# A hybrid decoder layer on one core: x tiles 2048 bytes apart, token sums for two units at a time, one weight sum by DMA, first gated tiles loaded under the up product

## The chip, the cores and the metric

The kernel runs on one core of a Trainium2 chip. TensorE (PE) multiplies, VectorE (DVE), ScalarE (ACT) and GpSimd (POOL) work on whole tiles, SyncE (SP) starts most DMAs. The metric is device time of one execution in microseconds, lower is better; the figure for a kernel is the median of its runs. A matmul's form is written "128*128 128x512": 128x128 weights against a moving tile of 128 rows and 512 columns.

## The reference

One layer, batch 1, 512 tokens, width 2048, all float32, in three sub-layers with a residual each: a mixer of three head groups, a cross-attention into 256 memory tokens, and a gated MLP with a causal convolution of width 3 over the gate. The change is in the seam from the second to the third, in the third, and in how the tiles of activations are laid out everywhere.

```python
def memory_cross_attention(h, mem_n, w_q, w_kv, w_o):
...
    o = jnp.einsum('bhsm,bmhd->bshd', p.astype(v.dtype), v).reshape(B, S, CROSS_WIDTH)
    return o @ w_o

def conv_ffn(h, w_up, conv_w, conv_b, w_down):
    S = h.shape[1]
    val, gate = jnp.split(h @ w_up, 2, axis=-1)
    gp = jnp.pad(gate, ((0, 0), (CONV_W - 1, 0), (0, 0)))
    g = conv_b
    for i in range(CONV_W):
        g = g + conv_w[i] * gp[:, i:i + S]
    return (jax.nn.silu(g) * val) @ w_down

...
        x = x + hybrid_mixer(rms_norm(x, norm_mix[l]), w_in[l], f_bias[l], rel_table,
                             c_gate_w2[l], c_gate_b[l], c_norm[l], w_out[l])
        x = x + memory_cross_attention(rms_norm(x, norm_cross[l]), mem_n, w_cq[l], w_ckv[l], w_co[l])
        x = x + conv_ffn(rms_norm(x, norm_ffn[l]), w_up[l], conv_w[l], conv_b[l], w_down[l])
    return rms_norm(x, norm_final)
```

The width of the MLP is 5504, that is 43 tiles of 128.

## The kernel before

**Three matmuls for one.** Every float32 operand is split into a hi and a lo part of a type that PE takes faster. `mm3` adds hi·hi (L352), hi weights · lo activations (L353) and lo weights · hi activations (L354) in PSUM. The hi part is an ACT copy, the lo part a DVE subtraction. For weights that is `split_weights` (ACT L313, DVE L314) or `weights` (ACT L338, DVE L339): a raw tile `wraw` of 128x1024 (512 KB; `WR` = 5 buffers) becomes two halves, each with one of `WS` = 5 buffers `whi` and `wlo`. An element-wise operation that PE waits for is therefore nearly always a split.

**Activations** are kept as 16 pairs of tiles `xhi`, `xlo` (`xslot`), 512 columns of 4 bytes, each tile padded to 528 columns, so that neighbours start 2112 bytes apart. Other pools hold `coh`/`col` (the attention's output) and `gh`/`gl` (some of the gated tiles) without padding, 2048 bytes apart.

**The w_co stage** (end of `cross()`): eight units u. Each loads 512 KB of weights, does two chains of 12 matmuls 128x512, adds the result to the residual stream (`resid`, DVE L959) and to the sums of squares (`square`, L983: ACT squares, DVE and POOL take turns in adding), and calls `token_sums(u)`.

**Strassen.** The up product is done by seven products of half-size blocks instead of eight. Per unit u, `token_sums` scales two tiles (y0, y1), takes their halves of 256 tokens as a11, a21, a12, a22, makes four sums of them (DVE L1150), and splits all seven (ACT L1159, DVE L1160), 128x256 each. That makes 56 tiles of [hi | lo]; 32 lie in the slots of `xhi` and `xlo`, the others in pools of their own as `sum`. A table `SHIFT` shifts each unit's content within its tile by 0 to 14 elements.

**`up()`**: 43 rounds f. A round loads four blocks of weights (b11, b12, b22, b21, 512 KB each), makes the weight sums in four DVE operations of 128x1024 (L1193, temporaries t1, t2), and does the products in the order 1, 6, 5, 7, 4, 2, 3, each with 24 matmuls 128x256 (8 units times 3), 168 in all. The results become `val` (the value half) and `gp` (the gate), the convolution and the gate follow on ACT and DVE (L1226 to L1229, then a multiplication, L1193), and the gated tile is stored to DRAM as `gd` (SP, L1232). In the first round the norm's factor `R` is worked out too.

**The down product** (`ffn()`): `load` reads a gated tile back (`graw`, SP L1250), splits it (ACT L1258, DVE L1259) into an x slot or into `gh`/`gl`; its first group of units uses tiles 0 to 3, in two units of 24 matmuls 128x512, then tiles 4 to 7 and so on.

**What sets the order.** Each engine takes its instructions in one order, which a scheduler fixes when the program is built, near the order of the code; an instruction that waits holds all behind it on its engine. SP's DMAs are such a queue too: a load that is behind a store which waits for its data starts after it.

Of the kernel before, what the change touches and what calls it, by code (L numbers as in the profile page):

```python
# [47 lines left out]
GB_SLOTS = 10  # L48
SHIFT = (0, 1, 2, 4, 6, 8, 12, 14)
LEVELS = (64, 32, 16, 8, 4, 2, 1)  # L50
# [161 lines left out]
class _Trunk:  # L212
# [774 lines left out]
    def cross(self):  # L987
# [127 lines left out]
        wx = self.pool(es_w, "wx", "right")  # L1115
        self.sums = []
        for u in range(8):
            w = self.weights(d["w_co"][u])
            pss = [self.acc(), self.acc()]
            for half in range(2):  # L1120
                for k in range(4):
                    wh, wl = w((half * 4 + k) * P, P)
                    self.mm3(pss[half], wh, wl, oT[k][0], oT[k][1], k == 0, k == 3)
                dt = 2 * u + half
                self.resid(dt, pss[half], self.x1[dt], sqs, lambda n: wx.tile([P, n], F32, name="xsqt", tag="xsqt", bufs=2))
            if u == 7:
                es_o.close()
                self.es_fa = ExitStack()
                sx = self.pool(self.es_fa, "fa", "left")
            self.sums.append(self.token_sums(u, sx, wx))  # L1130
        es_w.close()

    def token_sums(self, i, pool, tmp):

        nc = self.nc
        y = []
        for e in range(2):
            t = tmp.tile([P, S], F32, name="y%d" % e, tag="y%d" % e, bufs=2)
            nc.scalar.activation(t, self.x1[2 * i + e], AF.Copy, scale=self.gain(2, 2 * i + e))
            y.append(t)  # L1140
        a11, a21 = y[0][:, :HT], y[0][:, HT:]
        a12, a22 = y[1][:, :HT], y[1][:, HT:]
        s = [tmp.tile([P, HT], F32, name="s%d" % n, tag="s%d" % n, bufs=2) for n in range(1, 5)]
        src = {1: a11, 6: s[1], 5: s[0], 7: s[2], 4: a22, 2: a12, 3: s[3]}
        made = {5: (a21, a22, ALU.add), 6: (s[0], a11, ALU.subtract), 7: (a11, a21, ALU.subtract),
                3: (a12, s[1], ALU.subtract)}
        out = {}
        for n, j in enumerate((1, 5, 6, 7, 4, 2, 3)):
            if j in made:
                nc.vector.tensor_tensor(src[j], made[j][0], made[j][1], op=made[j][2])  # L1150
            slot = 7 * i + n
            if slot < 2 * KT:
                tag = ("xhi", "xlo")[slot % 2]
                t = self.xp.tile([P, S + 16], F32R, name=tag, tag=tag, bufs=KT)
            else:
                t = pool.tile([P, S + 16], F32R, name="sum%d" % slot)
            o = SHIFT[i]
            th, tl = t[:, o:o + HT], t[:, o + HT:o + S]
            nc.scalar.activation(th, src[j], AF.Copy)  # L1159
            nc.vector.tensor_tensor(tl, src[j], th.bitcast(F32), op=ALU.subtract)  # L1160
            out[j] = (th, tl)
        return out

    def up(self):

        nc, d = self.nc, self.d
        es = ExitStack()
        fb = self.pool(es, "fb", "right")  # L1170
        gps = [fb.tile([P, S + 2], F32, name="gp%d" % i) for i in range(2)]
        for g in gps:
# [5 lines left out]

        def raw(u):
            t = self.wp.tile([P, 1024], F32, name="wraw", tag="wraw", bufs=WR)  # L1180
            nc.sync.dma_start(out=t, in_=d["w_up"][u])
            return t

        def product(j, w, ps, start, stop):
            for h in range(2):
                th, tl = self.split_weights(w[:, h * 512:(h + 1) * 512])
                for k in range(4):
                    i, c = 4 * h + k, slice(k * P, (k + 1) * P)
                    self.mm3(ps, th[:, c], tl[:, c], *self.sums[i][j], start and i == 0, stop and i == NP - 1,
                             more=True)  # L1190

        def tt(out, a, b, op):
            nc.vector.tensor_tensor(out, a, b, op=op)  # L1193

        def one(f):
            b11, b12, b22, b21 = [raw(4 * f + i) for i in range(4)]
            pa, pb = self.acc()[:, :HT], self.acc()[:, :HT]
            pc, pd = self.pst("C")[:, :HT], self.pst("D")[:, :HT]
            s1, u2, u3 = [fb.tile([P, HT], F32, name=n, tag=n, bufs=1) for n in ("s1", "u2", "u3")]
            val = fb.tile([P, S], F32, name="val", tag="val", bufs=1)  # L1200
            gp = gps[f % 2]
            product(1, b11, pa, True, True)
            nc.scalar.activation(s1, pa, AF.Copy)
            t1 = fb.tile([P, 1024], F32, name="t1", tag="t1", bufs=1)
            t2 = fb.tile([P, 1024], F32, name="t2", tag="t2", bufs=1)
# [3 lines left out]
            tt(u2, pb, s1, ALU.add)  # L1209
            product(5, t1, pc, True, True)  # L1210
            if f == 0:
                self.R = self.rms(self.sqs, S, self.con)
            tt(b12, b22, b12, ALU.subtract)
            product(7, b12, pb, False, True)
            tt(u3, pb, s1, ALU.add)
            tt(gp[:, 2 + HT:], pc, u3, ALU.add)
            tt(t2, t2, b21, ALU.subtract)
            product(4, t2, pd, True, True)
            tt(val[:, hi], u3, pd, ALU.subtract)
            product(2, b21, pa, False, True)  # L1220
            nc.scalar.activation(val[:, lo], pa, AF.Copy)
            product(3, b22, pc, False, True)
            tt(gp[:, 2:2 + HT], pc, u2, ALU.add)
            tt(gp[:, 2:], gp[:, 2:], self.R, ALU.mult)
            c = fb.tile([P, S], F32, name="cv", tag="cv", bufs=2)
# [7 lines left out]

        self.gd = {}
        for f in range(FT):
# [5 lines left out]
    def ffn(self):  # L1241
# [3 lines left out]
        fp = self.pool(es, "fp", "right")  # L1245
        gT = {}

# [147 lines left out]
```

## Time and profile before

| | us |
|---|---|
| median of 3 runs | 2411.97 (2410.82 to 2414.61) |
| the profiled execution, whole | 2413.33 |
| its span in the trace | 2411.5 |
| mixer, and cross-attention up to its output product | 0 to 974.5 |
| w_co stage with token sums | 974.5 to 1032.2 |
| up(), 43 rounds | 1032.2 to 1904.9 |
| seam without matmuls | 1904.9 to 1914.2 |
| down product, end | 1914.2 to 2411.5 |

The clock that PE was granted is 0.991 of full on average. A row of the profile reads: line, engine, operation, output<-inputs with their form, count, then busy time and the mean of one in ns, then the idle time of the engine before them and what ended it. In a row of one tile, three durations stand for the least, the middle and the greatest in ns, then the first and the last start in us. In a timeline, a row has start, duration, engine and instruction; matmuls overlap, so that the next starts before the last ends, and their pace is read from start to start. PEld is the loading of weights beside the matmuls. DMA rows give KB and the median time from issue to landing.

### The profile page before, as it was taken

How to read it: one execution, taken by the hardware profiler on the slowest of the kernel's cores; microseconds unless marked ns; L12 is line 12 of the kernel's file. 1: busy time of each engine (PE TensorE's matmuls, PEld its weight loads, DVE VectorE, ACT ScalarE, POOL GpSimd, SP SyncE). 2: the span in 40 equal slices, each digit the busy share in tenths (PEclk: the TensorE clock that was granted, in tenths of full speed). 3: DMA queues.
4: the chain of work that ended last, by engine and by line, in shares of the span. 5: the costliest groups of instructions: out<-in, count | busy, mean ns of one | idle time of the engine just before them, and what ended most of it. 6: DMA issues, size and time to landing. Idle time of an engine off the chain costs nothing.

```text
span 2411.5 us, 37909 instructions
## 1 busy us (share of the span) xinstructions
PE 2360.5 (98%) x14514; PEld 2119.6 (88%) x14514; DVE 1657.7 (69%) x3112; ACT 1140.8 (47%) x2185; POOL 88.2 (4%) x91
## 2 busy tenths in 40 slices
PE   9999999999999999889999999999999899999997
PEld 8798898888878888689999999999999788888887
DVE  7726656667785365888888888888888733343336
ACT  6323346555664264655555555555555522232223
POOL 2000000000001000100000000000000000000003
PEclk9999999999999999989999999999999999999999
DMA  6432132222224352123333333333333533242332
GB/s 206 145 95 83 47 105 80 96 89 94 86 91 149 119 161 80 60 94 119 119 119 119 119 119 119 119 119 119 119 119 119 184 104 120 96 158 96 109 103 73
DMA packets 87458, 269.15 MB, mean 112 GB/s; under 512 B 9788, under 2 KB 14540, under 8 KB 87276
## 3 DMA queue, kind: packets, MB, share of 16 engines
q1 hardware_dynamic: 79504, 254.64, 32.9%
q10 hardware_dynamic: 7772, 12.09, 1.5%
q8 instruction: 114, 1.87, 0.3%
q14 instruction: 68, 0.56, 0.1%
HBM read 251.18 MB, written 19.45 MB: 112 GB/s over the span
## 4 chain that ended last, share of the span: by engine, by line
PE 93%; DVE 3%; ACT 2%; DMA 1%; POOL 1%; issue 0%; DVEq 0%; SPq 0%; POOLq 0%; ACTq 0%
PE acc L352 18%; PE acc L354 18%; PE acc L353 18%; PE psC L353 3%; PE psC L352 3%; PE psC L354 3%; PE acc L393 3%; PE acc L395 3%; PE acc L394 3%; PE psD L353 2%; PE psD L354 2%; PE psD L352 2%; PE psU L354 2%; PE psV L354 2%; PE psU L353 2%; PE psV L353 2%
## 5 line engine op out<-in xcount | busy, mean ns | idle before, releaser
L339 DVE TENSOR_TENSOR wlo<-wraw,whi 128x512 fp32r<-128x512 f32 (+2 forms) x496 | 336.8, 683 | 427.4 <-ACT whi L338 418.8
L338 ACT ACTIVATE whi<-wraw 128x512 fp32r<-128x512 f32 (+2 forms) x496 | 304.5, 617 | 643.5 <-PE acc L353 381.9
L352 PE MATMUL acc<-xhi,whi 128*128 128x512 f32 (+1 forms) x1518 | 554.4, 365 | 14.8 <-ACT xhi L1258 9.0
L354 PE MATMUL acc<-xhi,wlo 128*128 128x512 f32 (+1 forms) x1518 | 548.8, 362 | 0.0
L353 PE MATMUL acc<-xlo,whi 128*128 128x512 f32 (+1 forms) x1475 | 535.7, 363 | 0.0
L352 PEld LDWEIGHTS acc<-xhi,whi 128*128 128x128 f32 x1518 | 286.8, 189 | 56.6 <-ACT xhi L1258 9.2
L354 PEld LDWEIGHTS acc<-xhi,wlo 128*128 128x128 f32 x1518 | 287.4, 189 | 46.0 <-issue 0.8
L353 PEld LDWEIGHTS acc<-xlo,whi 128*128 128x128 f32 x1475 | 278.8, 189 | 43.5 <-issue 0.9
L313 ACT ACTIVATE whi<-wraw 128x512 fp32r<-128x512 f32 x344 | 215.7, 631 | 201.2 <-PE acc L353 70.3
L314 DVE TENSOR_TENSOR wlo<-wraw,whi 128x512 fp32r<-128x512 f32 x344 | 232.3, 686 | 34.0 <-ACT whi L313 32.7
L313 ACT ACTIVATE whi<-t 128x512 fp32r<-128x512 f32 x258 | 162.9, 633 | 160.2 <-PE acc L353 97.0
L314 DVE TENSOR_TENSOR wlo<-t,whi 128x512 fp32r<-128x512 f32 x258 | 173.5, 687 | 40.0 <-ACT whi L313 39.2
L352 PE MATMUL acc<-sum,whi 128*128 128x256 f32 x559 | 157.8, 282 | 0.9 <-ACT sum L1159 0.9
L353 PE MATMUL acc<-sum,whi 128*128 128x256 f32 x559 | 157.9, 283 | 0.5 <-DVE sum L1160 0.5
L354 PE MATMUL acc<-sum,wlo 128*128 128x256 f32 x559 | 157.3, 281 | 0.0
L353 PE MATMUL acc<-xhi,whi 128*128 128x256 f32 x430 | 121.6, 283 | 0.0
L393 PE MATMUL acc<-whi,xhi 128*128 128x384 f32 (+2 forms) x320 | 114.8, 359 | 1.0 <-ACT whi L338 0.6
L395 PE MATMUL acc<-whi,xlo 128*128 128x384 f32 (+2 forms) x320 | 112.6, 352 | 0.4 <-DVE xlo L306 0.4
L394 PE MATMUL acc<-wlo,xhi 128*128 128x384 f32 (+2 forms) x320 | 112.3, 351 | 0.0
L352 PE MATMUL acc<-xlo,whi 128*128 128x256 f32 x387 | 109.5, 283 | 0.0
L354 PE MATMUL acc<-xlo,wlo 128*128 128x256 f32 x387 | 109.3, 282 | 0.0
L353 PEld LDWEIGHTS acc<-sum,whi 128*128 128x128 f32 x559 | 106.0, 190 | 0.7 <-DVE sum L1160 0.7
(369 smaller groups left out, 5245.0 us busy)
## 6 DMA issues: line engine op xcount, KB each, us to landing
wraw<-in_w_up SPq DMA_DIRECT2D x172, 512.0 KB, 3.8
wraw<-in_w_dn SPq DMA_DIRECT2D x80, 512.0 KB, 3.7
wraw<-in_w_o SPq DMA_DIRECT2D x32, 512.0 KB, 3.6
wraw<-in_w_qka SPq DMA_DIRECT2D x24, 512.0 KB, 3.7
gd<-cv SPq DMA_DIRECT2D x43, 256.0 KB, 4.3
graw<-gd SPq DMA_DIRECT2D x43, 256.0 KB, 4.4
wraw<-in_w_qkb SPq DMA_DIRECT2D x16, 512.0 KB, 3.8
xraw<-in_xT SPq DMA_DIRECT2D x15, 512.0 KB, 3.8
```

Of the source, the lines that this page charges most:

```text
L313: nc.scalar.activation(hi, r, AF.Copy)
L314: nc.vector.tensor_tensor(lo, r, hi.bitcast(F32), op=ALU.subtract)
L338: nc.scalar.activation(hi, r, AF.Copy)
L339: nc.vector.tensor_tensor(lo, r, hi.bitcast(F32), op=ALU.subtract)
L352: nc.tensor.matmul(out, lh, rh, start=start, stop=False, skip_group_check=more)
L353: nc.tensor.matmul(out, lh, rl, start=False, stop=False, skip_group_check=more)
L354: last = nc.tensor.matmul(out, ll, rh, start=False, stop=stop, skip_group_check=more)
L393: self.nc.tensor.matmul(o, xh[:, tt], wh, start=(k == 0), stop=False)
L394: self.nc.tensor.matmul(o, xh[:, tt], wl, start=False, stop=False)
L395: self.last = self.nc.tensor.matmul(o, xl[:, tt], wh, start=False, stop=(k == KT - 1))
```

## The change

It has five parts.

1. `xslot` no longer pads: x tiles are 512 columns, 2048 bytes, apart. The table `SHIFT` becomes the constant 8, for the sums in pools of their own.
2. `token_sums` handles two units at once (v = 0 to 3, called after each odd u): y tiles of [128, 2, 512], sums and splits of 128x2x256. The sums are stored by product: `sums[j, v]` holds a hi tile and a lo tile with two units each. Products 1, 5, 2, 6 lie in the x slots, the others as `sh`/`sl` in pools. Some sums have another sign, and the results are combined accordingly. The w_co weights are split two units ahead.
3. After unit 6, the first two weight blocks of round 0 are loaded and b11 split; after unit 7, b11 + b12 is made and split, before the last token sums.
4. In `up()` the products run in the order 1, 5, 2, 6, 3, 4, 7. The weight sums are made in place: b11 += b12, += b22, += b21 on DVE, and b22 += b12 by an accumulating DMA from POOL's queue, which reads b12 again from DRAM, in two halves of 256 KB. b22 has two buffers of its own (pool `fb`).
5. In the last round, gated tiles 0 to 3 are read into two `wraw` buffers and split into x slots before the products end; `load` then starts with tile 4. The DMA scratch memory grows from 1024 to 2048 bytes.

```diff
@@
-        hi = self.xp.tile([P, n], F32R, name="xhi", tag="xhi", bufs=KT, padded_shape=[P, S + 16])
-        lo = self.xp.tile([P, n], F32R, name="xlo", tag="xlo", bufs=KT, padded_shape=[P, S + 16])
+        hi = self.xp.tile([P, n], F32R, name="xhi", tag="xhi", bufs=KT, padded_shape=[P, S])
+        lo = self.xp.tile([P, n], F32R, name="xlo", tag="xlo", bufs=KT, padded_shape=[P, S])
@@ cross(), the w_co stage
-            w = self.weights(d["w_co"][u])
+            w = ws[u]
...
+            if u + 2 < 8:
+                ws.append(self.weights(d["w_co"][u + 2]))
+            elif u == 6:
+                first = [self.up_raw(i) for i in range(2)]
+                self.first = [first, self.halves(first[0])]
+            else:
+                nc.vector.tensor_tensor(first[0], first[0], first[1], op=ALU.add)
+                self.first.append(self.halves(first[0]))
...
-            self.sums.append(self.token_sums(u, sx, wx))
+            if u % 2:
+                self.token_sums(u // 2, wx)
@@ token_sums
+        def part(j):
             if j in made:
                 nc.vector.tensor_tensor(src[j], made[j][0], made[j][1], op=made[j][2])
...
+            th, tl, o = self.sums[j, v]
+            th, tl = [t[:, o:o + S].rearrange("p (i c) -> p i c", c=HT) for t in (th, tl)]
             nc.scalar.activation(th, src[j], AF.Copy)
             nc.vector.tensor_tensor(tl, src[j], th.bitcast(F32), op=ALU.subtract)
...
+        for j in UP_ORDER:
+            part(j)
@@ new
+    def halves(self, w, add=None):
+
+        parts = []
+        for h in range(2):
+            c = slice(h * 512, (h + 1) * 512)
+            parts.append(self.split_weights(w[:, c]))
+            if add is not None:
+                self.nc.gpsimd.dma_start(out=w[:, c], in_=self.d["w_up"][add][:, c], accum_op=ALU.add)
+        return parts
@@ up(), one round
-            tt(t1, b12, b11, ALU.subtract)
-            tt(t2, b22, t1, ALU.subtract)
-            product(6, t2, pb, True, True)
...
+            if f:
+                tt(b11, b11, b12, ALU.add)
+                w5 = self.halves(b11)
+            product(5, w5, pc, True, True)
+            nc.scalar.activation(s5, pc, AF.Copy)
+            product(2, self.halves(b21), pa, False, True)
...
+            tt(b11, b11, b22, ALU.add)
+            product(6, self.halves(b11), pb, True, True)
...
+            product(3, self.halves(b22, 4 * f + 1), pc, False, True)
...
+            tt(b11, b11, b21, ALU.add)
+            product(4, self.halves(b11), pd, True, True)
+            if f == FT - 1:
+                self.early = [self.wp.tile([P, 2, S], F32, name="wraw", tag="wraw", bufs=WR) for _ in range(2)]
+                for i, t in enumerate(self.early):
+                    for k in range(2):
+                        nc.sync.dma_start(out=t[:, k, :], in_=self.gd[2 * i + k])
+            product(7, self.halves(b22), pb, False, True)
+            if f == FT - 1:
+                for i in range(FB):
+                    src = self.early[i // 2][:, i % 2, :]
+                    self.gT[i] = self.xslot()
+                    nc.scalar.activation(self.gT[i][0], src, AF.Copy)
+                    nc.vector.tensor_tensor(self.gT[i][1], src, self.gT[i][0].bitcast(F32), op=ALU.subtract)
```

How this moves instructions, at two places. A row is line, operation, output<-inputs and form; numbers behind a name tell tiles of one name apart. The lines are those of each kernel's own code: after the change, L1175 and L1179 are the sums and splits in `token_sums`, L316 the weight splits, L1227 the sums of weights and results.

DVE from the last unit's token sums to the first weight splits of `up()`, before:

```order
L1160 TENSOR_TENSOR sum_9950<-s_9942,sum_9950 128x256
L1160 TENSOR_TENSOR sum_9958<-s_9944,sum_9958 128x256
L1160 TENSOR_TENSOR sum_9954<-s_9943,sum_9954 128x256
L1160 TENSOR_TENSOR sum_9961<-y_9940,sum_9961 128x256
L1160 TENSOR_TENSOR sum_9964<-y_9940,sum_9964 128x256
L1150 TENSOR_TENSOR s_9945<-y_9940,s_9943 128x256
L1160 TENSOR_TENSOR sum_9968<-s_9945,sum_9968 128x256
L1193 TENSOR_TENSOR t_10028<-wraw 128x1024
L1193 TENSOR_TENSOR t_10029<-wraw,t_10028 128x1024
L1193 TENSOR_TENSOR wraw<-wraw 128x1024
L314 TENSOR_TENSOR wlo<-t_10029,whi 128x512 x2
L314 TENSOR_TENSOR wlo<-t_10028,whi 128x512 x2
```

The same place after the change, from the third split of the last pair of units on:

```order
L1179 TENSOR_TENSOR xlo<-y_9865,xhi 128x512
L1175 TENSOR_TENSOR sb<-sa,y_9862 128x512
L1179 TENSOR_TENSOR sl_9859<-y_9865,sh_9858 128x512
L1175 TENSOR_TENSOR sa<-y_9862 128x512
L1179 TENSOR_TENSOR xlo<-sb,xhi 128x512
L316 TENSOR_TENSOR wlo<-wraw,whi 128x512
L1175 TENSOR_TENSOR sb<-sb,y_9865 128x512
L1179 TENSOR_TENSOR sl_9861<-sa,sh_9860 128x512
L316 TENSOR_TENSOR wlo<-wraw,whi 128x512
L1179 TENSOR_TENSOR sl_9857<-sb,sh_9856 128x512
L1227 TENSOR_TENSOR wraw<-wraw,b_9892 128x1024
L316 TENSOR_TENSOR wlo<-wraw,whi 128x512 x2
```

Before, three operations of 128x1024 stand between the last sum and the splits of the weights that follow. After, one stands there, the sums are twice as wide, and two splits of a block that needs no sum stand among them.

SP from the last rounds of `up()` to the down product, before (`gd<-cv` stores of the last two rounds, `wraw<-in_w_dn` the down weights, `graw` the gated tiles read back, beginning with tile 0):

```order
L1181 DMA wraw<-in_w_up 128x1024
L327 DMA wraw<-in_w_dn 128x1024 x3
L1232 DMA gd_21001<-cv 128x512
L327 DMA wraw<-in_w_dn 128x1024 x4
L1232 DMA gd_21263<-cv 128x512
L1250 DMA graw<-gd_10259 128x512
L1250 DMA graw<-gd_10521 128x512
```

The same place after the change (`L1269` reads back tiles 0 to 3; the stores belong to the last three rounds, and `graw` begins with tile 4):

```order
L1269 DMA wraw<-gd_10156 128x512
L1288 DMA gd_20676<-cv 128x512
L1269 DMA wraw<-gd_10419 128x512
L1269 DMA wraw<-gd_10682 128x512
L1269 DMA wraw<-gd_10945 128x512
L329 DMA wraw<-in_w_dn 128x1024 x2
L1288 DMA gd_20939<-cv 128x512
L329 DMA wraw<-in_w_dn 128x1024 x6
L1288 DMA gd_21224<-cv 128x512
L329 DMA wraw<-in_w_dn 128x1024
L1306 DMA graw<-gd_11208 128x512
L1306 DMA graw<-gd_11471 128x512
```

Before, the first read of a gated tile stands behind the last store. After, four reads stand two stores earlier, and tile 4 stands behind the last store and one more load of down weights.

More of the change, by code (lines that the diff above doesn't have):

```diff
@@ L1142, in token_sums @@
[L1142 to L1148, printed above, removed]
+        a11, a21 = y[0][:, :, :HT], y[0][:, :, HT:]
+        a12, a22 = y[1][:, :, :HT], y[1][:, :, HT:]
@@ L1149, in token_sums @@
+        sa, sb = [tmp.tile([P, 2, HT], F32, name=n, tag=n, bufs=1) for n in ("sa", "sb")]
+        src = {1: a11, 2: a12, 4: a22, 5: sa, 6: sb, 3: sb, 7: sa}
+        made = {5: (a22, a21, ALU.subtract), 6: (sa, a11, ALU.add), 3: (sb, a12, ALU.subtract),
+                7: (a21, a11, ALU.subtract)}
+        def part(j):
             if j in made:
                 nc.vector.tensor_tensor(src[j], made[j][0], made[j][1], op=made[j][2])
[L1151 to L1156, printed above, removed]
@@ L1177, in cw, with product @@
             return self.conv[:, i * FT + f:i * FT + f + 1]
[L1179 to L1190, printed above, removed]
+        def product(j, parts, ps, start, stop):
+            for i in range(NP):
+                th, tl = parts[i // 4]
+                c = slice(i % 4 * P, (i % 4 + 1) * P)
+                sh, sl, o = self.sums[j, i // 2]
+                m = slice(o + i % 2 * HT, o + (i % 2 + 1) * HT)
+                self.mm3(ps, th[:, c], tl[:, c], sh[:, m], sl[:, m], start and i == 0, stop and i == NP - 1, more=True)
@@ L1197, in one @@
             pa, pb = self.acc()[:, :HT], self.acc()[:, :HT]
             pc, pd = self.pst("C")[:, :HT], self.pst("D")[:, :HT]
[L1199 to L1200 removed]
+            s1, s5, u2, u3 = tmp("s1"), tmp("s5"), tmp("u2"), tmp("u3")
+            val = tmp("val", S, 2)
             gp = gps[f % 2]
[L1202 removed]
+            if f:
+                w1 = self.halves(b11)
```

82 lines of the change are left out of this document (50 added, 32 removed).

## The prediction

> **What bounds the kernel now.** I read first the page's busy times and its chain, then a table by stretch of time, and last the single gaps.
>
> ```profile
> PE 2360.5 (98%) x14514; PEld 2119.6 (88%) x14514; DVE 1657.7 (69%) x3112; ACT 1140.8 (47%) x2185; POOL 88.2 (4%) x91
> PE 93%; DVE 3%; ACT 2%; DMA 1%; POOL 1%; issue 0%; DVEq 0%; SPq 0%; POOLq 0%; ACTq 0%
> ```
>
> PE is busy for 98% of the span and holds 93% of the chain. So time can come from two places: from the pitch of the matmuls (start to start, with nothing between), or from the few stretches in which PE waits. The table by stretch shows the second kind.
>
> ```profile
> core 0: us, PE busy (x) PEld busy (x) DVE busy (x) ACT busy (x) POOL busy (x), PEclk, DMA share, GB/s
> 974.50:1032.20 57.70, 46.76 (x182) 35.73 (x182) 52.32 (x111) 39.21 (x88) 12.60 (x8) 0.91 0.17 55
> 1032.20:1064.20 32.00, 24.53 (x174) 23.45 (x173) 29.02 (x48) 18.76 (x35) 1.44 (x3) 0.84 0.24 77
> 1064.20:1084.20 20.00, 20.00 (x171) 20.00 (x170) 17.74 (x28) 11.69 (x19) 0.00 (x0) 1.00 0.38 127
> 1904.90:1914.20 9.30, 0.31 (x4) 0.10 (x2) 4.10 (x8) 4.03 (x6) 0.00 (x0) 0.73 0.49 167
> ```
>
> The first row is the `w_co` stage, the second the first of the 43 rounds of `up()`, the third a settled round, the fourth the seam between `up()` and the down product. In a settled round PE is never idle. In the first two stretches DVE is busy for 81.34 of 89.70 us while PE idles for 18.4 of them and the granted clock falls to 0.91 and 0.84: DVE is the bound there. At the seam no engine is: 9.3 us pass in a chain of short steps.
>
> **The change, part by part.**
>
> *(a) x tiles 2048 bytes apart.* The trace has both layouts side by side in the down product: `xhi`/`xlo` lie 2112 bytes apart before, `gh`/`gl`, from another pool, 2048.
>
> ```profile
> L352 PE MATMUL psU<-gh,whi x40: 388/389/397, 1966.8 to 2338.4; 128*128 128x512 f32 x40
> L352 PE MATMUL psU<-xhi,whi x120: 387/393/399, 1922.4 to 2356.5; 128*128 128x512 f32 x120
> ```
>
> ```profile
> 1995.65 0.39 PE L354 MATMUL acc<-gh,wlo 128*128 128x512 f32 x1
> ...
> 1999.73 0.39 PE L354 MATMUL acc<-gh,wlo 128*128 128x512 f32 x1
> ...
> 2000.18 0.40 PE L353 MATMUL psU<-xlo,whi 128*128 128x512 f32 x1
> ...
> 2011.54 0.39 PE L354 MATMUL psU<-xhi,wlo 128*128 128x512 f32 x1
> ```
>
> From 1995.65 to 1999.73 lie 18 pitches on `gh`/`gl`: 226.7 ns each. From 2000.18 to 2011.54 lie 49 on `xhi`/`xlo`: 231.8 ns. The medians (the middle of the three durations) differ by 4 ns, 389 against 393, the pitches by 5. How many matmuls have such tiles:
>
> ```profile
> L352 PE MATMUL acc<-xhi,whi 128*128 128x512 f32 x1056 | 423.7, 401 | 9.0 <-ACT xhi L1258 9.0
> L354 PE MATMUL acc<-xhi,wlo 128*128 128x512 f32 x1056 | 418.0, 396 | 0.0
> L353 PE MATMUL acc<-xlo,whi 128*128 128x512 f32 x1056 | 417.3, 395 | 0.0
> L352 PE MATMUL psV<-xhi,whi 128*128 128x512 f32 x120 | 47.2, 393 | 0.0
> ```
>
> That is 3168, and with 120 on each of three lines for both `psU` and `psV`, 3888. At 4 ns they give 15.6 us. The least duration on `xhi`, 387, says that some run at the short pitch already, so I take **14**. The ends: nothing, if the pool and not the spacing makes the difference; 19.8 at 5.1 ns. A loss is possible too: in the new layout a hi tile and its lo tile are exactly 32768 bytes apart, a distance that no row of before shows; by the gap between the two layouts I bound it at 14 us the other way.
>
> A page speaks against this term. The Trainium skill, "TensorE: Matmul & The Clock Gate", section "Part 2: What happens when you issue a matmul", gives the matmul's moving operand and the weight load independent read ports and a fixed 216 ns between 512-wide matmuls, so spacing should not count; the trace has 226.7 and 231.8 instead of one figure. By that rule the term would be 0.
>
> *(b) Token sums in pairs of units, and the first weights before them.* Per unit, DVE before has 2 residual adds, 2 weight splits, on average 0.9 adds of squares, and 11 sums and splits 256 wide.
>
> ```profile
> L959 DVE TENSOR_TENSOR str<-acc,str 128x512 f32<-128x512 f32 x7 | 4.7, 684 | 2.0 <-PE acc L354 2.0
> L1160 DVE TENSOR_TENSOR sum<-s,sum 128x256 fp32r<-128x256 f32 x9 | 3.6, 416 | 0.0
> ```
>
> Over eight units: 39 operations of 512 at 0.684 and 88 of 256 at 0.416, 63.3 us, against 192 matmuls at 0.227, 43.6, on PE. After: 39 + 44 of 512, all at 0.684, 56.8. DVE remains the bound and saves **6.5**. Then the start of `up()`:
>
> ```profile
> 1035.76 0.38 PE L352 MATMUL acc<-sum,whi 128*128 128x256 f32 x1 [0.92 <-ACT sum L1159]
> 1036.64 0.38 PE L353 MATMUL acc<-sum,whi 128*128 128x256 f32 x1 [0.50 <-DVE sum L1160]
> 1036.86 0.28 PE L354 MATMUL acc<-sum,wlo 128*128 128x256 f32 x1
> 1042.95 0.58 PE L352 MATMUL acc<-xhi,whi 128*128 128x256 f32 x1 [5.81 <-ACT whi L313]
> ```
>
> ```profile
> L1193 DVE TENSOR_TENSOR t<-wraw 128x1024 f32<-128x1024 f32 x43 | 52.8, 1227 | 1.4
> L1160 DVE TENSOR_TENSOR sum<-s,sum x13: 411/414/426, 1015.7 to 1039.4; 128x256 fp32r<-128x256 f32 x13
> 1040.00:1048.00 8.00, 4.80 (x20) 4.51 (x21) 7.97 (x10) 4.16 (x7) 0.00 (x0) 0.50 0.20 66
> ```
>
> The last split of a sum starts at 1039.4; behind it on DVE stand three weight sums of 1.23 us (3.7 in all), which product 6 needs, and PE stands still for 5.81 us, then runs at half clock (0.50 from 1040 to 1048). In the changed order the splits of products 1 and 5 are done before the last sums, the sums come in the order in which products use them, and product 2 needs no weight sum. The first round took 32.0 where a settled one takes 20.0. What is late next are the last four units' worth of sums, 11 operations of 0.684 or 7.5 us behind the last residual add, of which product 1 needs the first only and each later product 2.9 us later. I leave 5.5 of the 12.0 us standing and take **6.5**. Together (b) is 13. The ends: nothing (DVE gains nothing by wide operations), and 26.1, which is all that both stretches hold: 89.7 less 43.6 less 20.0.
>
> *(c) Weight sums in place, one by DMA.* The pace of a settled round:
>
> ```profile
> L352 PE MATMUL psD<-xhi,whi x86: 278/280/281, 1055.6 to 1897.1; 128*128 128x256 f32 x86
> ACT whi L313 <- PE acc L353: 156.7, 194, 0.8
> L1193 DVE TENSOR_TENSOR gp<-gp,R x43: 684/686/694, 1066.4 to 1905.7; 128x512 f32<-128x512 f32 x43
> L1228 DVE SCALAR_TENSOR_TENSOR cv<-gp,conv,cv x43: 743/746/752, 1070.1 to 1908.0; 128x512 f32<-128x512 f32 x43
> ```
>
> From 1055.6 to 1897.1 are 42 rounds, 20.04 us each: 168 matmuls at 119.3 ns. ACT, which feeds them, waits for PE to free a weight buffer (156.7 us on that row alone, from 1100 to 1900), so PE sets the pace. Per round the change takes one weight sum (1.23 us) from DVE, exchanges the 0.69 of `gp<-gp,R` for a 0.75 operation of the kind in the last row, and gives ACT one more 256-wide copy. All of it lies under PE: **0**. Only a new pitch of the 256-wide matmuls could move it; 1.2 ns either way would be 9 us over 7224 matmuls, and that is the end I keep. The DMA on POOL's queue is a new wait. Half n of `b22` is issued after DVE's split of it in product 3 and read again four halves later, in product 7. A half is 12 matmuls, 1.43 us; ACT sees the DMA after 3 halves, 4.3 us, and PE, with three halves of lead in the five buffers, after 8.6.
>
> ```profile
> wraw<-in_w_up SPq DMA_DIRECT2D x172, 512.0 KB, 3.8
> graw<-gd SPq DMA_DIRECT2D x43, 256.0 KB, 4.4
> ```
>
> No such transfer is in the trace. The nearest rows land in 3.8 and 4.4 us; I take 4.4 for 256 KB, hence nothing, and keep as the bad end twice that, 8.8, since it reads its target as well. The Trainium skill, "DMA: Bandwidth & Descriptors", section "Anatomy of one DMA — SWDGE (gpsimd) path", has 2.0 us plus the bytes by 436 GB/s, an estimate of 2.6 us here, for plain transfers; by it the term is 0 as well, and no run here shows it yet.
>
> *(d) Four gated tiles under up.*
>
> ```profile
> 1904.89 0.28 PE L354 MATMUL psC<-sum,wlo 128*128 128x256 f32 x1
> 1914.16 0.80 PE L352 MATMUL acc<-xhi,whi 128*128 128x512 f32 x1 [8.99 <-ACT xhi L1258]
> ...
> 1919.32 0.42 PE L354 MATMUL acc<-xhi,wlo 128*128 128x512 f32 x1
> ```
>
> ```profile
> 1910.19 0.33 SPq L1232 DMA_DIRECT2D gd<-cv  x1
> 1910.57 4.61 SPq L1250 DMA_DIRECT2D graw<-gd  x8
> ...
> 1913.48 1.31 ACT L1258 ACTIVATE xhi<-graw 128x512 fp32r<-128x512 f32 x2 [2.74 <-DMA graw<-gd]
> ...
> L1258 ACT ACTIVATE xhi<-graw 128x512 fp32r<-128x512 f32 x30 | 18.3, 626 | 6.7 <-DMA graw<-gd 4.9 <-PE psV L354 1.2
> L1259 DVE TENSOR_TENSOR xlo<-graw,xhi 128x512 fp32r<-128x512 f32 x30 | 20.2, 690 | 6.7 <-ACT xhi L1258 6.6
> ```
>
> PE stands from 1905.01 to 1914.16 because the loads of the gated tiles stand behind the last round's store in SP's queue, and then does 12 matmuls in 5.16 us, at half clock, where 12 × 0.232 is 2.8. That is 9.15 + 2.4 = 11.5. After, tiles 0 to 3 wait ready, which is 48 matmuls or 11 us of work at 0.23. Tile 4 decides what is left. In SP's order one more load of down weights now stands between the last store and tile 4. It takes the fifth-last `wraw` buffer, which is free once the eighth half of down weights is split, and that split needs a `whi` buffer that PE gives up after three halves, 36 matmuls or 8.3 us into the down product. With 0.6 and 0.7 us of splitting, tile 4's load starts some 9.7 us after `up()` ends, lands 2.9 later as the first `graw` did (issued at 1910.57, ACT's wait for it over at 1913.48) and needs 0.63 more until PE can begin: 13.2 to 14.7 with the median landing of 4.4, against the 11.0 that are covered. PE stands for 2.2 to 3.7 us and may run a few matmuls at half clock. I leave 4.5 of the 11.5 standing, 3 of idling and 1.5 of low clock, and take **7**; ends 0 and 11.5.
>
> The two loads per round more (0.5 MB beside 2.5) and the larger DMA scratch get nothing: SP's loads are issued a round ahead.
>
> **Sum.** Against the profiled execution, 2413.3 (span 2411.5 and 1.8 around it; the median of the runs, 2412.0, is 1.3 less): 2413.3 − 14 − 13 − 0 − 7 = **2379**.
>
> **Rivals.**
> 1. *Spacing buys nothing.* For it: `gh` and `xhi` are also of different pools. Against: PE does the same instructions at the same weights within 5 us of each other. Then 2413.3 − 20 = 2393. The rule of the Trainium skill, "TensorE: Matmul & The Clock Gate", quoted under (a) has the same result.
> 2. *DVE stays the bound of the seam into up.* For it: DVE at 52.32 of 57.70 us, and still 56.8 of work to do; the first weights' splits now stand ahead of the last sums. If half of (b) comes, 2386; if none, 2392.
> 3. *The accumulating DMA is late.* PE loses in each of 43 rounds what the transfer takes over 8.6 us. Place: ACT's split of `b22` in product 7. The other gains, 34, are used up at 34 / 43 = 0.8 us, so from 9.4 us on the kernel is slower; at 10 us it takes 2379 + 60 = 2439. Against it: every load on the page lands in under 5.
> 4. *The change does not do what it says*, because another wait stands at each of the three places: about 2410.
>
> **How the numbers follow.** Forecast 0.60; rival 1, 0.18; rival 2, 0.11; rival 3, 0.09; rival 4, 0.02. The range: at the low end (a) gives 19.8, (b) 20, (d) 11.5, or 2362; at the high end stand rivals 1 and 2 together, with half of (b), 2400. The 9 us of a new pitch in (c) would count only where all else is at its end, so it widens each by 2: 2360 to 2402. It leaves out rivals 3 and 4 and little else. Faster or slower by 0.2% (4.8 us) is about what a measurement of this kernel can tell from no change: faster 0.89 (the forecast and rivals 1 and 2), same 0.02 (rival 4), slower 0.09 (rival 3).
>
> **What would show it.** (a) `psU<-xhi` at a median of 389 like `gh`, pitch 227. (b) `w_co` in 51 us instead of 57.7, the first round in about 25.5, no gap over 3 us at its second product. (c) rounds of 20.04, no wait of ACT or PE for a DMA into `b22`. (d) no gap before the down product, one of 2 to 4 us some 11 us into it, at tile 4. Wrong would be, above all, rounds that are longer or shorter than 20.04, since each 0.1 us of them is 4.3 us.

## The result, and the profile after

The changed kernel takes **2521.9 us** (median of 4 runs, 2516.2 to 2523.4) against 2412.4 of the kernel before: 1.0449 times as long, 95% interval 1.0431 to 1.0467. Slower was forecast with a chance of 0.09; the range given was 2360 to 2402. The profiled execution has a span of 2514.5 us.

By stage, in us, from the first and last matmuls of each in the traces (the last column is a kernel of the experiments: the one before with new spacing only):

| | before | after | spacing only |
|---|---|---|---|
| `w_co` begins | 968.8 | 960.1 | 961.9 |
| `up()` begins | 1032.2 | 1011.6 | 1024.5 |
| `up()` lasts | 872.7 | 1008.8 | 874.5 |
| no matmul until down begins | 9.3 | 0.1 | 9.2 |
| down and end last | 497.3 | 493.9 | 490.1 |

`w_co` is taken here from its first matmul, 968.8 before; the table ahead of the prediction cuts it at 974.5, behind the last matmuls of the attention, which are mixed with its first. So every other stage became shorter, and `up()` 136 us longer. The page of the changed kernel: busy times, DMA queues, the chain, and the DMA issues.

```profile
PE 2401.5 (96%) x14514; PEld 2155.6 (86%) x14514; DVE 1593.1 (63%) x3025; ACT 1112.3 (44%) x2200; POOL 163.0 (6%) x177
...
q1 hardware_dynamic: 79504, 254.64, 30.1%
q0 software_dynamic: 12384, 22.55, 6.2%
...
PE 31%; DMA 10%; DVE 7%; issue 6%; ACT 2%; POOL 2%; ACTq 0%; DVEq 0%; POOLq 0%
DMA b<-in_w_up 10%; PE acc L356 7%; PE acc L354 6%; PE acc L355 6%; DVE wlo L316 3%; ACT whi L315 2%; PE psU L354 1%; PE psV L354 1%; PE psU L355 1%; PE psU L356 1%; PE psV L355 1%; PE psV L356 1%; DVE wraw L1227 1%; POOL b L1201 1%; DVE cv L1284 1%
...
wraw<-in_w_up SPq DMA_DIRECT2D x129, 512.0 KB, 5.4
...
b<-in_w_up POOLq DMA_DIRECT2D x86, 256.0 KB, 6.0
```

PE's share of the chain fell from 93% to 31%: something else now ends last, and the largest single entry is the DMA into `b`. The last row is that DMA, the accumulating b22 += b12; it lands in a median of 6.0 us, both halves together, where 4.4 was assumed. The waits of ACT and PE say who notices (the first two lines are ACT's, the third is PE's):

```profile
ACT whi L315 <- DMA b<-in_w_up: 240.5, 74, 6.1
ACT whi L315 <- DVE wraw L1227: 127.7, 92, 2.9
...
PE acc L354 <- ACT whi L315: 63.0, 39, 3.2
```

ACT's split of b22 waits for that DMA 74 times, 240.5 us in all. Three rounds in the table by stretch, cut from one product 4 to the next:

```profile
1504.26:1528.99 24.73, 22.07 (x171) 21.65 (x169) 16.39 (x26) 10.11 (x19) 1.75 (x2) 0.93 0.43 125
1528.99:1552.55 23.56, 22.08 (x171) 21.66 (x169) 16.39 (x26) 10.17 (x20) 1.77 (x2) 0.93 0.46 134
1552.55:1572.95 20.40, 20.30 (x170) 20.10 (x169) 16.38 (x26) 10.04 (x19) 1.76 (x2) 1.00 0.44 116
```

Each was 20.0 before, with PE busy throughout. DVE is busy for 16.4 us of a round and ACT for 10, so neither is full. Over some 40 such rows the mean round is 23.2 us: PE idles for 1.8 of it and loses 0.85 to a lower granted clock (the 0.93 of two of these rounds); the other 0.5 is in neither. One round in the timeline, POOL's issues first, then ACT and PE:

```profile
1500.46 0.87 POOL L1201 DMA_DIRECT2D b<-in_w_up  x1 [19.85 <-DVE wlo L316]
1502.80 0.87 POOL L1201 DMA_DIRECT2D b<-in_w_up  x1 [1.47 <-DVE wlo L316]
...
1505.62 0.63 ACT L315 ACTIVATE whi<-b 128x512 fp32r<-128x512 f32 x1 [2.84 <-DMA b<-in_w_up]
1510.45 0.63 ACT L315 ACTIVATE whi<-b 128x512 fp32r<-128x512 f32 x1 [4.20 <-DMA b<-in_w_up]
...
1511.13 0.38 PE L354 MATMUL acc<-sh,whi 128*128 128x256 f32 x1 [2.44 <-ACT whi L315]
```

The first half, issued at 1500.46, is used at 1505.62; the second, issued at 1502.80, at 1510.45, 7.65 us later. ACT stands for 2.84 and 4.20 us, with everything behind it in its order, and PE then for 2.44.

### The profile page after: what moved, and what is told of

The parts are those of the page before. It is cut to its first block, busy times and chain, and to the rows that moved or that the text cites. A ratio compares the mean times of both kernels' runs of the same rounds, so it can differ in the third digit from the quotient of the medians.

```text
span 2514.5 us, 38340 instructions
## 1 busy us (share of the span) xinstructions
PE 2401.5 (96%) x14514; PEld 2155.6 (86%) x14514; DVE 1593.1 (63%) x3025; ACT 1112.3 (44%) x2200; POOL 163.0 (6%) x177
## 3 DMA queue, kind: packets, MB, share of 16 engines
q1 hardware_dynamic: 79504, 254.64, 30.1%
q0 software_dynamic: 12384, 22.55, 6.2%
## 4 chain that ended last, share of the span: by engine, by line
PE 31%; DMA 10%; DVE 7%; issue 6%; ACT 2%; POOL 2%; ACTq 0%; DVEq 0%; POOLq 0%
DMA b<-in_w_up 10%; PE acc L356 7%; PE acc L354 6%; PE acc L355 6%; DVE wlo L316 3%; ACT whi L315 2%; PE psU L354 1%; PE psV L354 1%; PE psU L355 1%; PE psU L356 1%; PE psV L355 1%; PE psV L356 1%; DVE wraw L1227 1%; POOL b L1201 1%; DVE cv L1284 1%
## 5 line engine op out<-in xcount | busy, mean ns | idle before, releaser
L354 PE MATMUL acc<-xhi,whi 128*128 128x256 f32 (+1 forms) x2120 | 731.7, 345 | 11.0 <-ACT xhi L1314 4.0
L356 PE MATMUL acc<-xhi,wlo 128*128 128x256 f32 (+1 forms) x2120 | 722.7, 341 | 2.7 <-DVE wlo L316 2.7
L355 PE MATMUL acc<-xlo,whi 128*128 128x256 f32 (+1 forms) x2120 | 722.2, 341 | 0.0
L354 PEld LDWEIGHTS acc<-xhi,whi 128*128 128x128 f32 x2120 | 411.8, 194 | 54.8 <-ACT s L1248 9.5
L356 PEld LDWEIGHTS acc<-xhi,wlo 128*128 128x128 f32 x2120 | 410.2, 193 | 46.4 <-DVE wlo L316 3.5
L355 PEld LDWEIGHTS acc<-xlo,whi 128*128 128x128 f32 x2120 | 411.3, 194 | 39.0 <-issue 0.8
L316 DVE TENSOR_TENSOR wlo<-wraw,whi 128x512 fp32r<-128x512 f32 x430 | 281.1, 685 | 35.0 <-ACT whi L315 34.9
L316 DVE TENSOR_TENSOR wlo<-b,whi 128x512 fp32r<-128x512 f32 x172 | 118.1, 688 | 253.1 <-ACT whi L315 251.7
L315 ACT ACTIVATE whi<-b 128x512 fp32r<-128x512 f32 x172 | 107.1, 624 | 281.1 <-DMA b<-in_w_up 240.5
L354 PE MATMUL acc<-sh,whi 128*128 128x256 f32 x344 | 107.9, 314 | 63.3 <-ACT whi L315 63.0
L356 PE MATMUL acc<-sh,wlo 128*128 128x256 f32 x344 | 109.8, 319 | 8.6 <-DVE wlo L316 8.2
L1227 DVE TENSOR_TENSOR wraw<-wraw 128x1024 f32<-128x1024 f32 x85 | 103.7, 1220 | 1.5
```

The lines of the kernel that those rows point to most:

```text
L315: nc.scalar.activation(hi, r, AF.Copy)
L316: nc.vector.tensor_tensor(lo, r, hi.bitcast(F32), op=ALU.subtract)
L354: nc.tensor.matmul(out, lh, rh, start=start, stop=False, skip_group_check=more)
L355: nc.tensor.matmul(out, lh, rl, start=False, stop=False, skip_group_check=more)
L356: last = nc.tensor.matmul(out, ll, rh, start=False, stop=stop, skip_group_check=more)
```

## The experiments

Every kernel was timed beside the kernel before on the same chip; "rounds" are steady rounds of `up()` in its trace.

**1. Without the sum.** Edit to the changed kernel:

```diff
-            product(3, self.halves(b22, 4 * f + 1), pc, False, True)
+            product(3, self.halves(b22), pc, False, True)
```

> Leaves out the sum b22 += b12 altogether (product 7 then uses b22 alone), so no accumulating DMA and nothing in its place. Theory L (the late DMA holds ACT, and that is all): rounds of 20.0 us, 2376 to 2386 in all. Rival S (the weight sums in place make a chain of ACT and DVE steps too long for a round, DMA or not): rounds stay above 20.5, over 2430.

Measured: 2381.7 us (ratio 0.987, 0.9851 to 0.989), rounds of 20.05. This kernel leaves the sum out, so product 7 uses b22 alone. All of the loss comes with the DMA, and the sums in place are not in themselves too long a chain. Theory S falls.

**2. The sum on DVE.**

```diff
-            product(3, self.halves(b22, 4 * f + 1), pc, False, True)
+            product(3, self.halves(b22), pc, False, True)
+            tt(b22, b22, b12, ALU.add)
```

> The same sum as a fourth DVE operation of 128x1024, 1.22 us, in the place of the DMA. L: DVE has the room (16 of 20 us busy), rounds of 20.0 us, 2376 to 2388. S: longer rounds than without the sum, over 2440.

Measured: 2385.0 us (0.9887, 0.987 to 0.9903), rounds of 20.05, the first interval between rounds 21.5. DVE had the room.

**3. Product 3 ahead of product 6, with the DMA.**

```diff
             tt(b11, b11, b22, ALU.add)
+            product(3, self.halves(b22, 4 * f + 1), pc, False, True)
             product(6, self.halves(b11), pb, True, True)
             tt(u2, s1, pb, ALU.subtract)
-            product(3, self.halves(b22, 4 * f + 1), pc, False, True)
```

> Keeps the DMA and puts product 3 ahead of product 6, so that two more halves, 2.9 us, lie between the issue and the use. L: ACT now sees only what a transfer takes over 7.2 us, rounds of 20.0 to 20.5, 2376 to 2405. S: rounds as long as after the change, 2500 or more.

Measured: 2381.2 us (0.987, 0.9855 to 0.9885), rounds of 20.02. The transfers landed in a median of 4.7 us, and from 1100 to 1850 us ACT waits for one of them once, for 1.1 us; PE never does.

**4. Spacing alone, on the kernel before.** `xslot` without padding, and the sums that lie in x slots without a shift.

```diff
-        hi = self.xp.tile([P, n], F32R, name="xhi", tag="xhi", bufs=KT, padded_shape=[P, S + 16])
+        hi = self.xp.tile([P, n], F32R, name="xhi", tag="xhi", bufs=KT, padded_shape=[P, S])
...
-                t = self.xp.tile([P, S + 16], F32R, name=tag, tag=tag, bufs=KT)
+                t = self.xp.tile([P, S], F32R, name=tag, tag=tag, bufs=KT)
...
-            o = SHIFT[i]
+            o = SHIFT[i] if slot >= 2 * KT else 0
```

> The kernel before with the x tiles 2048 bytes apart and nothing else. If the spacing sets the pitch of the 512-wide matmuls: 227 ns in place of 232, 2412 - 14 = 2398 (2394 to 2401). If it is the pool, or another part of the change: 2412.

Measured: 2401.2 us against 2411.7 (0.9952, 0.9937 to 0.9966): 10.5 us. The row of the down product's matmuls in this kernel:

```profile
L352 PE MATMUL psU<-xhi,whi x120: 389/389/389, 1916.7 to 2343.0; 128*128 128x512 f32 x120
```

The median went from 393 to 389, what `gh` had before, and even the longest is 389. So the spacing sets the pitch, not the pool. By the stage table, 6.9 us of it lie ahead of `w_co`, and 7.2 in the down product, in the profiled execution; the rounds became 0.04 us longer, 1.7 in all; why is not known.

**5. A sixth pair of weight buffers.** Experiments 1 to 3 showed that it was the DMA, but the lead of 8.6 us was not what protects PE, since 7.65 was already too late. My next theory was a closed loop, K: from the split of b22 in product 3 through its DMA to its split in product 7, and through ACT's and DVE's work on to the next product 3. Every sixth half gets a pair of its own from pool `fb`; `val` has one buffer and u3 shares u2's, to make room.

```diff
-            parts.append(self.split_weights(w[:, c]))
+            parts.append(self.split_more(w[:, c]) if self.more else self.split_weights(w[:, c]))
...
-            s1, s5, u2, u3 = tmp("s1"), tmp("s5"), tmp("u2"), tmp("u3")
-            val = tmp("val", S, 2)
+            s1, s5, u2, u3 = tmp("s1"), tmp("s5"), tmp("u2"), tmp("u2")
+            val = tmp("val", S, 1)
```

> The changed kernel with a sixth pair of weight buffers in the rounds (val has one buffer and u3 shares u2's, to make room). Theory K (a closed loop of ACT, DVE and the DMA, from the split of b22 in product 3 through its sum to product 7 and on to the next product 3, is longer than a round; buffers are filled once and don't shorten it): rounds still 22.5 to 23.8 us, 2495 to 2535. Rival B (as the prediction had it, PE loses what a transfer takes over the lead that the buffers give): one half more of lead, 1.43 us less per round, 2440 to 2465.

Measured: 2447.6 us (1.014, 1.012 to 1.016), rounds of 21.6. K's number is wrong, and rival B's is right. Three of its rounds:

```profile
1495.58:1516.65 21.07, 20.52 (x170) 20.15 (x169) 16.56 (x26) 10.12 (x19) 1.77 (x2) 1.00 0.50 139
1516.65:1537.89 21.24, 20.75 (x170) 20.20 (x169) 16.56 (x26) 10.11 (x19) 1.76 (x2) 1.00 0.49 138
1537.89:1559.11 21.22, 20.60 (x170) 20.21 (x169) 16.56 (x26) 10.11 (x19) 1.75 (x2) 1.00 0.49 136
```

PE idles for 0.85 us of a round in place of 1.8, and in no round is the clock lowered.

**6. The control: the same without the sixth pair.**

```diff
-            s1, s5, u2, u3 = tmp("s1"), tmp("s5"), tmp("u2"), tmp("u3")
-            val = tmp("val", S, 2)
+            s1, s5, u2, u3 = tmp("s1"), tmp("s5"), tmp("u2"), tmp("u2")
+            val = tmp("val", S, 1)
```

> The changed kernel with val in one buffer and u3 sharing u2's, as in the run with a sixth pair of weight buffers, but with five pairs. If the sixth pair shortened the rounds there: 2510 to 2530 and rounds of 23 us. If it was the other edits (order and landing of the transfers): 2440 to 2455, rounds of 21.5.

Measured: 2519.1 us (1.0435, 1.0385 to 1.0486), rounds of 23.1. It is the buffer that shortens a round by 1.5 us.

**7. Product 7 ahead of product 4: two halves less between issue and use.**

```diff
-            tt(b11, b11, b21, ALU.add)
-            product(4, self.halves(b11), pd, True, True)
+            product(7, self.halves(b22), pb, False, True)
...
-            product(7, self.halves(b22), pb, False, True)
+            tt(b11, b11, b21, ALU.add)
+            product(4, self.halves(b11), pd, True, True)
```

> The changed kernel with product 7 ahead of product 4, so that two halves, 2.9 us, less lie between the issue of the DMA and the use. Law K2 (a round is 20.0 us and what a transfer takes from issue to use over ACT's slack, 4.3 us after the change, and no buffer absorbs any of it): slack 1.4, rounds of 24.5 to 26.5, 2570 to 2660. Rival B (PE loses what is over 8.6 us, here over 5.7): rounds under 22, below 2490.

Measured: 2517.7 us (1.043, 1.0399 to 1.046), rounds of 23.2, as after the change. Both expectations are wrong: neither the halves between issue and use, counted at PE's pace, nor what exceeds them sets the length of a round.

**8 and 9. Half of b22 by DMA, half on DVE.** First the first half, then in a kernel of its own the second; the two differ in one number.

```diff
-            if add is not None:
+            if add is not None and h == 0:
                 self.nc.gpsimd.dma_start(out=w[:, c], in_=self.d["w_up"][add][:, c], accum_op=ALU.add)
+            elif add is not None:
+                self.nc.vector.tensor_tensor(w[:, c], w[:, c], b[:, c], op=ALU.add)
```

The first half by DMA (h == 0):

> Only the first half of b22 is summed by DMA, the second by DVE (128x512). K: the first transfer landed 5.1 us after its issue, the second 7.6, so the loop through the first is some 11.5 + 0.4 + 5.1 = 17 us, under a round: rounds of 20.0 to 20.3, 2380 to 2395. Rival P (any transfer from POOL's queue stops ACT for several us): rounds of 21 or more, over 2420.

Measured: 2385.9 us (0.9884, 0.9865 to 0.9904), rounds of 20.05. The second half by DMA (h == 1):

> The changed kernel with the first half of b22 summed on DVE and only the second by DMA. If the second transfer took 7.2 us because it is in line behind the first: it now takes 4.8 to 5.2 from issue to use, the loop of 13 + 2.7 + 5 is near a round, rounds of 20.0 to 20.8, 2380 to 2415. If it is the loads on SP's queue that run at that later time: 6.5 or more, rounds of 22 or more, over 2460.

Measured: 2543.3 us (1.0545, 1.0514 to 1.0575), rounds of 24.0. With half as many transfers it is slower than the changed kernel, so the second transfer is not late because it stands behind the first. One round of the kernel with the first half by DMA (POOL, SP, ACT):

```profile
1499.27 0.89 POOL L1201 DMA_DIRECT2D b<-in_w_up  x1 [19.14 <-DVE wlo L316]
...
1500.11 0.33 SPq L1191 DMA_DIRECT2D wraw<-in_w_up  x1
1500.67 0.33 SPq L1290 DMA_DIRECT2D gd<-cv  x1
1502.48 0.93 SPq L1191 DMA_DIRECT2D wraw<-in_w_up  x2
...
1504.03 1.15 ACT L315 ACTIVATE whi<-b 128x512 fp32r<-128x512 f32 x2 [1.89 <-DMA b<-in_w_up]
```

And of the kernel with the second:

```profile
1508.65 0.33 SPq L1191 DMA_DIRECT2D wraw<-in_w_up  x1
1509.09 0.37 SPq L1290 DMA_DIRECT2D gd<-cv  x1
1509.55 2.09 SPq L1191 DMA_DIRECT2D wraw<-in_w_up  x2
...
1510.45 0.88 POOL L1201 DMA_DIRECT2D b<-in_w_up  x1 [22.61 <-DVE wlo L316]
...
1517.83 0.63 ACT L315 ACTIVATE whi<-b 128x512 fp32r<-128x512 f32 x1 [7.49 <-DMA b<-in_w_up]
```

In the first, the transfer is issued 0.8 us ahead of SP's burst (three loads of 512 KB and a store of 256 KB) and used 4.8 us later; in the second, 1.8 us after its beginning, and used 7.4 us later. It is the same 256 KB. Counted from the packets, SP's queue moves 0.33 MB while the first is under way (1499.27 to 1503.8) and 1.72 MB while the second is (1510.45 to 1517.7). In the first kernel ACT stands for 1.9 us in the round shown, for 49.9 us in 23 rounds between 1100 and 1850, and PE still never waits.

**10. One DMA for both halves.** The call leaves the loop over the halves and takes all of w.

```diff
-            if add is not None:
-                self.nc.gpsimd.dma_start(out=w[:, c], in_=self.d["w_up"][add][:, c], accum_op=ALU.add)
+        if add is not None:
+            self.nc.gpsimd.dma_start(out=w, in_=self.d["w_up"][add], accum_op=ALU.add)
```

> The changed kernel with both halves summed by one DMA of 512 KB, issued after the second split. If the time of such a transfer goes with its bytes (two of 256 KB took 10 us between them, 2.3 times the engine time per byte of plain loads): 8 to 10 us until use, rounds of 23.5 to 26, 2530 to 2640. If it is a fixed cost for each: 5 to 6 us, rounds of 20.5 to 21.5, 2400 to 2445.

Measured: 2577.5 us (1.0687, 1.0656 to 1.0718), rounds of 24.8, 8.2 us from issue to use. The forecast by bytes met the number, but its rule is not shown: experiment 9 issues half the bytes at the same place and needs 7.4, so twice the bytes cost 0.8 us more (SP's queue moves 1.2 MB beside them, 1.6 in experiment 9, in the mean). One transfer is the worse choice, since all of it is issued late.

**11 and 12. A faster kernel.** Product 3 ahead of 6, and `need` asks for tiles 4 to 7 at the first block:

```diff
-                need((b + 1) * FB)
+                need((b + 1 + (b == 0)) * FB)
```

> Product 3 ahead of 6 with the DMA, and the reads of gated tiles 4 to 7 asked for before the first down weights in the code. If tile 4's read waits on SP behind a load of down weights, the gap of 4.0 us at the second block goes: 2381 - 4 to 6 = 2375 to 2377. If it waits for the last store alone: 2381.

Measured: 2381.5 us (0.9865, 0.9851 to 0.988): no gain, because the order on SP stayed as it was. Its rows are 1893.87 for the last store, 1896.00 for the load of down weights and 1896.38 for tile 4, and PE still waits 3.5 us. Then the same with the sum as in experiment 2:

> The same, with the sum b22 += b12 on DVE. If the DMA only takes work off an engine that has room: the same time within 0.2%, 2375 to 2379. If DVE is near its limit in the first round: 1 to 2 us more.

Measured: **2379.1 us** (0.9856, 0.9839 to 0.9872), the lowest median of all, 142.9 us below the changed kernel's. Its four runs (2378.8 to 2380.0) lie below those of experiment 11 beside it (2380.3 to 2382.2), though the intervals of the two ratios overlap. So the DMA earns nothing that DVE could not give.

## Why the prediction was wrong

**(c), the step that failed.** The prediction put the accumulating DMA at nothing, with two numbers: it lands in 4.4 us, like a plain load, and PE sees only what exceeds 8.6 us, the time of six halves. Both fail here, the second more so.

*Landing.* From issue to use it is 5.0 us on average for the first half and 7.2 for the second, inside the range that the prediction kept (up to 8.8), and below its threshold. By the queues on the page it costs 6.2% of the DMA engines' time for 22.55 MB, where plain loads cost 30.1% for 254.64 MB: 2.3 times as much for a byte. And it is late where SP's loads are issued ahead of it (experiments 8 and 9). The packets in the traces say the same. Means of some 37 rounds: a transfer lands in 4.2 us beside 0.01 MB of SP's queue (experiment 3, first half), in 4.9 beside 0.33 (after the change, first half), in 5.8 beside 0.65 (sixth pair, second half), in 7.1 beside 1.31 (after the change, second half) and in 7.3 beside 1.61 (experiment 9). In experiment 7, where the second follows the first by 0.6 us, it takes 6.1 beside 0.43, so SP's loads are not all of it. The 4.4 was thus no bad figure for the transfer alone; what it left out is the loads beside it. These were not taken away in any run, so that they are the cause rests on the pair and on these means; and whether a plain load from POOL's queue would be as late was not tried.

*The threshold.* The 4.3 us that ACT was to have were not there even at PE's pace. Without the DMA (experiment 1) product 7's second split begins 5.5 us after product 3's second, and 2.1 to 2.7 us pass from that split until its DMA is issued (second column below), where one half, 1.43, was counted: that leaves 2.8 to 3.4. The other 4.3 us, the lead of the buffers, are a stock that is spent once. When ACT has been held in one round, it does the following splits without waiting for PE: it is ready for product 7 2.7 us after product 3's second split begins, 3.3 in experiment 1. After a few rounds the length of a round is that of a loop: product 3's second split, its DMA, product 7's second split, and the splits and sums from there to the next product 3. From the starts in the traces, means of some 37 rounds, in us:

| | use to next split | split to issue | issue to use | round |
|---|---|---|---|---|
| after the change | 13.3 | 2.7 | 7.2 | 23.2 |
| product 7 ahead of 4 | 14.2 | 2.8 | 6.2 | 23.2 |
| second half only | 13.3 | 3.3 | 7.4 | 24.0 |
| one DMA | 13.9 | 2.7 | 8.2 | 24.8 |
| sixth pair of buffers | 12.2 | 3.5 | 5.9 | 21.6 |
| product 3 ahead of 6 | 11.6 | 2.1 | 6.4 | 20.0 |

In the row "one DMA" it is product 7's first split that counts. The columns add up to the round by construction, so the table alone proves no loop. For it speaks that the first column is 13.3 in two kernels whose DMAs differ, that experiments 9 and 10 came out as forecast from it (24.0 where 22 or more was forecast, 24.8 where 23.5 to 26 was), and experiment 3. Against it stand its two earlier forms, K and K2, which failed in experiments 5 and 7. With 13.3 and 2.7 spent, a transfer has 4.0 us until the round is longer than PE's 20.02. (The prediction's 20.04 reads a row with two starts per round as if it had one.) In experiment 7 the first column grew by 0.9 us and the transfer became 1.0 faster, hence no change. In experiment 3 one product was moved out of the first column, into the wait, and the loop fits. The last row is PE's pace: the waits for PE are in its columns.

What stays partly open is experiment 5. K said that buffers don't count, and they do: the first column fell by 1.1 us and the landing by 1.3. The first column holds waits of ACT for PE to free a buffer (83.0 us in 40 rounds after the change), of which K took no account, and PE runs them off faster where its clock isn't lowered. Whether the buffer acts through these was not tried. That the transfers landed sooner goes with less traffic beside them: with the sixth pair the second is issued 1.3 us after the first in place of 2.3, and SP's queue moves 0.65 MB during it in place of 1.31. Rival B met the number, but not by its rule: that rule gives no loss at 7.2 us.

Of the rivals it was the third that came true, with its place right (the split of b22 in product 7) and its decisive point, 9.4 us, wrong: the kernel was already slower at 7.2.

**(a), right in kind:** 10.5 us alone against 14, which is within the interval of 8 to 15. The medians moved as forecast, 393 to 389.

**(b), 13 forecast:** against spacing alone, with the rounds repaired (experiment 3), `w_co` until `up()` begins takes 51.5 us in place of 62.6, 11 us less where 6.5 were expected; the first round gained nothing where 6.5 were expected: `up()` less 42 rounds is 31.9 us before and 32.9 now. PE's gaps at the start of the first round of that kernel and in it:

```profile
1012.85 0.36 PE L354 MATMUL acc<-xhi,whi 128*128 128x256 f32 x1 [2.03 <-ACT sh L1178]
1015.64 0.58 PE L356 MATMUL acc<-xhi,wlo 128*128 128x256 f32 x1 [2.32 <-DVE wlo L316]
1020.43 0.38 PE L354 MATMUL psC<-xhi,whi 128*128 128x256 f32 x1 [1.15 <-ACT whi L315]
1022.06 0.39 PE L356 MATMUL psC<-xhi,wlo 128*128 128x256 f32 x1 [1.13 <-DVE wlo L316]
1029.01 0.41 PE L354 MATMUL acc<-xhi,whi 128*128 128x256 f32 x1 [1.84 <-ACT s L1248]
```

Before, the gaps in the first round sum to 7.5 us, 5.81 of it in one; now one of 2.0 stands at its start and four that sum to 6.4 in it. DVE is busy for 29.0 of its first 32 us in both kernels: the backlog is the same work, and PE arrives earlier at it. The sum of the term, 10, is near the 13 by luck, since its two halves missed in opposite directions.

**(d), 7 forecast, 6.3 found,** and by its own steps. In the kernel of experiment 3, `up()` ends at 1886.6; SP's rows and PE's gap:

```profile
1894.12 0.33 SPq L1288 DMA_DIRECT2D gd<-cv  x1
1896.24 0.33 SPq L329 DMA_DIRECT2D wraw<-in_w_dn  x1
1896.62 9.62 SPq L1306 DMA_DIRECT2D graw<-gd  x12
...
1901.73 0.73 PE L354 MATMUL acc<-xhi,whi 128*128 128x512 f32 x2 [4.02 <-ACT xhi L1314]
```

Tile 4's load starts 10.0 us after `up()` ends, 9.7 was forecast, behind the load of down weights; the gap is 4.0 where 2.2 to 3.7 was. The gap of 9 us is gone: the seam, down and end take 493.1 us, where the kernel with spacing alone takes 499.4.

With (c) at nothing, the kernels of experiments 1 to 3 take 2381 to 2385 us, where 2379 was forecast for this sum.

## What to carry to other kernels

Ask of an asynchronous step not only how long its result is waited for, but whether its wait closes a loop from one round to the next; if so, add up the whole loop, with the work between use and next start, and compare it with the round. Buffers and lead counted at the pace of the engine that is now the bound don't settle that: the sixth pair took 1.5 us off a round and left it 1.5 over PE's pace. Before a sum moves to a DMA, look whether the engine that has it is full (DVE was busy for 17.7 of 20 us before, and with the sum back on it in experiments 2 and 12 PE never waits in a settled round), and where other queues issue their loads.

## What the runs showed of the hardware

- An accumulating DMA of 256 KB into SBUF took 4.8 to 7.4 us from issue to use where something waited for it, by the traffic of SP's queue beside it, and landed in 4.2 with almost none, where the Trainium skill, "DMA: Bandwidth & Descriptors", section "Anatomy of one DMA — SWDGE (gpsimd) path", leads to an estimate of 2.6 us for plain transfers. POOL itself is busy for only 0.87 us of it; in experiments 3 and 8 the first packet of a first half moves 1.6 us after its issue.
- 512-wide matmuls run at a median of 389 ns in place of 393 once neighbouring x tiles are 2048 and not 2112 bytes apart; the rule of independent read ports in the Trainium skill, "TensorE: Matmul & The Clock Gate", section "Part 2: What happens when you issue a matmul", does not show this.
- Gaps of PE cost clock as well, and short ones do. In the settled rounds after the change the clock record of the trace shows the granted clock falling 19 times to half, for 3.41 us each (twice for 6.83), each time once a single gap of PE, of 1.26 to 3.23 us in all, had begun; no gap under 1.2 us went with it, and seven of 1.36 to 2.04 us did not. With a sixth pair of buffers no single gap in these rounds is over 1.0 us, and the clock never falls. Over all rounds the clock added about half of what the idling cost, 0.85 us beside 1.8.
